# A hybrid decoder step: the chained sum of a gated unit gets a PSUM tile of its own, and its seven products another order

## The chip, the cores and the metric

The kernel runs on one core of one Trainium2 chip. Its time is the device time of one execution in microseconds; a kernel is run several times and the median counts. TensorE (matmuls), VectorE, ScalarE, GpSimd and SyncE (transfers) each work through a queue of their own in order, and wait for each other with semaphores. TensorE writes its sums to PSUM, which has eight banks; VectorE and ScalarE read them there.

## What is computed

One step of a trunk of two layers for 560 tokens (16 meta tokens, 32 of running sequences, 512 of a new prompt), in float32. The model is 1024 wide, the hidden width is 2816:

```python
def swiglu(x, w_gate, w_up, w_down):
    return (jax.nn.silu(x @ w_gate) * (x @ w_up)) @ w_down
...
for l in range(DEPTH):
    h = h + 0.5 * swiglu(rmsnorm(h, norm_ffn1[l]), ffn1_w_gate[l], ffn1_w_up[l], ffn1_w_down[l])
    m, a, b, c = mixer(rmsnorm(h, norm_mix[l]), l, ...)   # HGRN2 heads and an S5 state-space part
    h = h + m
    h = h + 0.5 * swiglu(rmsnorm(h, norm_ffn2[l]), ffn2_w_gate[l], ffn2_w_up[l], ffn2_w_down[l])
return rmsnorm(h, norm_final), ...
```

So there are four FFN stages and two mixers: FFN, mixer, FFN, FFN, mixer, FFN.

## The kernel before, in words

Every float32 product is made of three products of reduced-precision halves: a value is split into a high part and the rest, and high x high, high x low and low x high are summed (`mms`, line 397; the matmuls `mm<-xh,wh`, `xl,wh`, `xh,wl` of the profile). The low part of a weight comes from a copy with the sign turned and a transfer that adds the weight from HBM onto it (`wl<-in_gu_dram` on GpSimd's queue).

An FFN stage has 22 units of 128 hidden features each (`Unit`, line 804). Gate and up product of a unit together are a 2 x 2 block product over halves of the tokens and halves of the inputs, done with seven block products in place of eight (`PROD`, line 801; the operands are sums and differences that `t_wsum` and `Norm.t_blocks` make). Each of the seven is 12 matmuls of 280 columns (272 in the last stage): four groups of three. The sums 1, 6, 7 and 4 are one chain in bank 0 of the unit's tile `x` (`mm` in the profile, two banks): after 1, 6 and 7 ScalarE copies the running sum to SBUF (`t_cuts`, line 841: `s1`, `u2`, `u3`), and the next product adds on to it in place. Products 5 and 3 are a second chain in bank 1 of the same tile, with the copy `s5` between them. Product 2 has a one-bank tile `c` of its own (`m` in the profile). `t_hid` (line 851) puts gate (`f`, tile `fa`) and up (`b`, tile `s`) together, multiplies them by the row scale of the norm, applies Silu, multiplies and splits.

The order of TensorE's products is written out in `ffn` (line 984): within a unit 6, 2, 3, 7, then products 1 and 5 of the next unit, then 4. After each chunk of 4 or 6 units (`CH`) the down product of the chunk follows: eight output tiles, each 24 matmuls for a chunk of four, with `t_res` (VectorE, `h<-mm,h`) adding the result to `h`.

All else is a list scheduler in Python that runs when the kernel is built (`Sched`, line 131). Tasks are generators that yield operations; the scheduler keeps estimated clocks, knows each operation's estimated cost, and emits the operation with the earliest start, with a pull by the task's priority and a `slack` that holds back a task's operations. What it emits is each engine's program order; the semaphores are then put in by the framework. For the tiles of two PSUM banks it kept its dependences per bank (`keys`, line 87, and `Pool.banks`). PSUM tiles come from two pools: `mm`, three tiles of two banks (`am()`), and `m1`, two tiles of one (`am1()`); a task that asks for a tile waits for a free one.

Two other tasks matter here. `Norm.t_sum` makes the row scale of a stage (squares on ScalarE, sums on VectorE or GpSimd, `rstd_of`, line 652); it runs while the first units are already on TensorE. `t_setup(l)` (line 1116) computes the S5 tables of layer l on the side, with low priority, during the FFN stages; the S5 part of the mixer (`t_s5`) sends `u` through HBM (`su<-u`, `ut<-su`) only once that setup is done (`yield d.ev`), and `x0` in the mixer's order waits for all four S5 outputs.

Of the kernel before, what the change touches and what calls it, by code (L numbers as in the profile page):

```python
# [12 lines left out]
AF = mybir.ActivationFunctionType  # L13
# [70 lines left out]
        self.pool, self.w, self.dt, self.name = pool, w, dt, name  # L84


def keys(a):

    n = a.tensor.name
    if a.ap[0][0] != 1024 or a.space != PSUM:  # L90
        return [n]
    lo = a.offset % 1024
    hi = lo + sum(st * (c - 1) for st, c in a.ap[1:])
    return [f"{n}/{b}" for b in range(lo // 512, hi // 512 + 1)]


class Op:
    __slots__ = ("eng", "cost", "outs", "ins", "fn", "lat", "alt", "bias", "port")

    def __init__(self, eng, cost, outs, ins, fn, lat=None, port=False):  # L100
        self.eng, self.cost, self.fn, self.alt, self.bias = eng, cost, fn, None, 0.0

        self.port = port
        self.lat = LAT[eng] if lat is None else lat
        self.outs = [n for a in outs for n in keys(a)]
        self.ins = [n for a in ins for n in keys(a)]


class Pool:
    def __init__(self, tp, shape, n, tag):  # L110
        self.tp, self.shape, self.tag = tp, shape, tag
        self.free = [0.0] * n
        self.n = n
        self.banks = tag == "gmm"


class Task:
# [13 lines left out]
class Sched:  # L131
# [20 lines left out]
    def free(self, *aps):  # L152
        for a in aps:
            n = a.tensor.name
            p = self.owner.pop(n)
            if n in self.wnames:
                self.wnames.discard(n)
                self.wheld -= 1
            ks = [n, f"{n}/0", f"{n}/1"] if p.banks else [n]
            p.free.append(max(d.get(k, ("", 0.0))[1] for k in ks for d in (self.wt, self.rt)))  # L160

    def step(self, t, val=None):
        try:
# [27 lines left out]
    def settle(self):  # L191
        again = True
        while again:
            again = False
            for t in list(self.tasks):
                while t in self.tasks:
                    c = t.cur
                    if c is None and not t.started:
                        self.step(t)
                    elif isinstance(c, Ev):  # L200
                        if not c.done:
                            break
                        self.step(t)
                    elif isinstance(c, Req):
                        p = self.pools[c.pool]
                        if len(p.free) <= self.reserve(t, c.pool):
                            break
                        p.free.sort()
                        tm = p.free.pop(0)
                        if c.pool == "a" and t.need:  # L210
                            t.took += 1
                        if c.pool == "a" and t.weights is not None:
                            self.wheld += 1
                        ap = p.tp.tile(p.shape, c.dt, tag=p.tag, name=c.name)
# [4 lines left out]
                        for k in [n, f"{n}/0", f"{n}/1"] if p.banks else [n]:  # L219
                            self.rt[k] = ("", tm)  # L220
# [48 lines left out]
    def run(self):  # L269
        self.settle()  # L270
        while self.tasks:
            best = {}
            for t in self.tasks:
# [10 lines left out]
                        o.alt.alt = None  # L284
                b = best.get(o.eng)
                key = st + PULL.get(o.eng, 0.0) * t.prio
                if t.slack and o.eng == "PE":
                    key = max(key, rdy + t.slack)
                if b is None or key < b[2] - 1e-9:
                    best[o.eng] = (st, t, key)  # L290
# [9 lines left out]
def hymba(ctx: ExitStack, tc: tile.TileContext, *aps):  # L300
# [35 lines left out]
    def tt(o, a, b, op, eng=None):  # L336
        if eng is ANY:
            return flex(tt(o, a, b, op), tt(o, a, b, op, G))
        e = eng or V
        c = nel(o) * 1.04 + 65 if e is V else nel(o) * 2.1 + 147  # L340
        return Op("V" if e is V else "G", c, [o], [a, b], lambda: e.tensor_tensor(o, a, b, op=op), port=sb(a, b))  # L341

    def flex(a, b, bias=BIAS):
# [305 lines left out]

    def rstd_of(acc, n, T=TOK):
        W = T // 2
        ps = yield am1()
        accs = acc if isinstance(acc, list) else [acc]
        yield mms([(ps[64 * j:64 * j + 64, 0, :W], ones, a[:, W * j:W * (j + 1)], a is accs[0], a is accs[-1])
                   for a in accs for j in range(2)])
# [21 lines left out]
        rs = yield al("rs", w=T)  # L679
        S = T // 2 if T > NH else T  # L680
        for o in range(0, T, S):
            ps = yield am1()
# [9 lines left out]
    class Norm:  # L692
        def __init__(self, nm, l, src, ev, o0=0):
# [9 lines left out]
            else:  # L703
                self.xs = [Ev() for _ in range(KD)]
                spawn(self.t_split(), 2.931, name="split" + nm)
            spawn(self.t_sum(), 8.533, name="sum" + nm).slack = 1500.0 if self.fast else 0.0

        def source(self, k):
            if self.src[k] is None:
# [62 lines left out]
        def t_sum(self):  # L772
            acc = None
            for k in range(KD):
# [5 lines left out]
                    yield add(q, q, acc, ANY)  # L780
                    free(acc)
                acc = q
            self.rs.val = yield from rstd_of(acc, D, self.T)
            self.rs.done = True

        def drop(self):
# [16 lines left out]

    class Unit:
        def __init__(self, nrm, f, k):
            self.i = unit_at[f, k]
            self.nrm, self.W = nrm, nrm.T // 2
            self.x = self.c = None
            self.pe = [Ev() for _ in range(8)]
            self.got = {k: Ev() for k in ("s1", "s5", "u2", "u3")}  # L810
            self.left = {"G": 2, "A": 2, "B": 2, "U": 1}
            self.out = Ev()

        def prod(self, j):
            w, o, b = PROD[j]
            q, i = wq[self.i], self.i
            if j == 1:
                self.x = yield am()
                spawn(t_cuts(self), 2.45, name="cuts")
                spawn(t_hid(self), 2.452, name="hid")  # L820
            if j == 2:
                self.c = yield am1()
            wait = {6: "s1", 3: "s5", 7: "u2", 4: "u3"}.get(j)
            if wait:
                yield self.got[wait]
            yield q.done[w]
            wh, wl, tiles = q.val[w]
            out = self.c[:, 0, :self.W] if j == 2 else self.x[:, 1 if j in (3, 5) else 0, :self.W]
            onto = wait is not None
            for k in range(4):  # L830
                e = self.nrm.xb[b][k]
# [6 lines left out]
            if not self.left[w]:  # L838
                free(*tiles)

    def t_cuts(t):
        W = t.W
        for j, nm, n, c, o in ((1, "s", "s1", 0, 0), (5, "s", "s5", 1, W), (6, "u", "u2", 0, 0), (7, "u", "u3", 0, W)):
            yield t.pe[j]
            if o == 0:
                t.val = yield al(nm, w=2 * W)
                setattr(t, nm, t.val)
            yield acopy(t.val[:, o:o + W], t.x[:, c, :W])
            t.got[n].done = True

    def t_hid(t):
        T, W = t.nrm.T, t.W
        a_, b_ = slice(0, W), slice(W, T)
        yield t.pe[2]
        f = yield al("fa", w=T)
        yield add(f[:, a_], t.c[:, 0, :W], t.s[:, a_])
        free(t.c)
        yield t.pe[3]
        yield add(f[:, b_], t.x[:, 1, :W], t.u[:, a_])
        yield t.nrm.rs  # L860
        rs = t.nrm.rs.val
        yield mul(f, f, rs)
        yield act(f, f, AF.Silu)
        yield t.got["u3"]
        b = t.s
        yield add(b[:, b_], t.u[:, b_], b[:, b_])
        free(t.u)
        yield mul(b[:, b_], b[:, b_], rs[:, b_])
        yield t.pe[4]
        yield mul(b[:, a_], t.x[:, 0, :W], rs[:, a_])  # L870
        free(t.x)
        yield mul(f, f, b)
        free(b)
        t.out.val = yield from split(f)
# [109 lines left out]
    def ffn(nrm, f, nm2, l2=0):  # L984
        us = [Unit(nrm, f, k) for k in range(FT)]
        prog = []
        for u in range(FT):
            if not u or u in ends:
                prog += [(u, 1), (u, 5)]
            if u + 1 in ends:  # L990
                prog += [(u, j) for j in (6, 2, 7, 3, 4)] + [(None, ends.index(u + 1))]
            else:
                prog += [(u, j) for j in ((2, 6, 3, 7) if u == 0 else (6, 2, 3, 7))] + [(u + 1, 1), (u + 1, 5), (u, 4)]
        hids = [u.out for u in us]
        for u, j in prog:
            if u is not None:
# [119 lines left out]
    def t_setup(l):  # L1116
# [76 lines left out]
        ps = yield am1()  # L1193
        yield trs([(ps[:, 0, 0:128], q8)])
        qt = small("qt", 128)
        yield acopy(qt, ps[:, 0, 0:128])
# [62 lines left out]
        pw = [bc[:, 512:1024], p1[:, 0:512], p1[:, 512:1024], p2[:, 0:512], p2[:, 512:1024]]  # L1259
        for n in range(4):  # L1260
            yield from cmul16(pw[n + 1], ar, ai, pw[n])
        ht, zt = xt[:, 0:512], xt[:, 512:1024]
        ps = yield am1()
        for mt in range(4):
            for c in range(2):
# [9 lines left out]
                yield mms([(ps[32 * jj:32 * jj + 32, 0, 128 * mt:128 * mt + 128],  # L1275
                            be[:, 512 * c + 128 * mt + 32 * jj:512 * c + 128 * mt + 32 * jj + 32],
                            ce[:, 160 * jj:160 * jj + 128], c == 0, c == 1) for jj in range(4)])
        free(bc, p1, p2, be)
        yield acopy(ht, ps[:, 0])
        free(ps)  # L1280
# [11 lines left out]
        free(xt)  # L1292

        es = [small(f"es{n}", 32) for n in range(10)]
        yield vcopy(es[0], un)
# [653 lines left out]
```

## Time and profile before

| | |
|---|---|
| median of 3 runs | 2375.29 us (2368.11 to 2376.02) |
| profiled execution | 2368.96 us, span 2367.2 us |
| TensorE busy | 2123.0 us, 17370 matmuls |
| TensorE's mean granted clock | 0.976 of full speed |

The span is what the profiler saw of the execution; 1.8 us lie around it. In the rows below times are microseconds, of one instruction nanoseconds; "PE" is TensorE's matmuls, "PEld" its weight loads, DVE VectorE, ACT ScalarE, POOL GpSimd, SPq SyncE's queue. `mm<-xh,wh` means: the instruction writes tile `mm` and reads `xh` and `wh`. "[0.61 <-DVE fa]" is idle time just before the instruction and what ended it. In the timelines each row begins with its start and its duration, and neighbours of one kind are merged (x12).

### The profile page before, as it was taken

Reading aid. Unit: us, or ns where it says so; the run is one execution under the profiler, and the core shown is the slowest. Engines: PE = TensorE matmul, PEld = TensorE weight load, DVE = VectorE, ACT = ScalarE, POOL = GpSimd, SP = SyncE. Lnnn points to the kernel's source line nnn. Section 1 sums busy time; section 2 is a strip of 40 time slices with the busy share of each in tenths; the row PEclk is TensorE's granted clock in tenths of the full one; section 3 lists DMA queues with packets and bytes.
Section 4 is the critical chain, followed back from the end, with each engine's and each line's share of the span. In section 5 each row is a group of like instructions: output and inputs, shape, how many; then the busy total and the mean of one; then the engine's idle time right before and its main releaser. Section 6 shows DMA issues by size and latency. Waiting matters only on the chain.

```text
span 2367.2 us, 43934 instructions
## 1 busy us (share of the span) xinstructions
PE 2123.0 (90%) x17370; PEld 2029.0 (86%) x17370; DVE 1632.5 (69%) x3647; ACT 1171.7 (49%) x1898; POOL 522.4 (22%) x623
## 2 busy tenths in 40 slices
PE   5899999998799899999979999999988989999997
PEld 4888898997689898989979988889878888888987
DVE  8867767868568876856888765555677776556564
ACT  6455555443355544565554554454425455544553
POOL 3122222322222122223221211112311231111111
PEclk9999999999899999999999999999989999999998
DMA  6677776986566567776747775678855647656663
GB/s 180 136 192 173 165 202 157 230 238 175 126 153 160 140 148 205 174 178 173 178 99 173 191 173 138 142 171 223 217 145 131 173 103 172 160 144 143 157 142 87
DMA packets 153615, 388.63 MB, mean 164 GB/s; under 512 B 16208, under 2 KB 36464, under 8 KB 153408
## 3 DMA queue, kind: packets, MB, share of 16 engines
q0 software_dynamic: 66048, 177.80, 39.7%
q1 hardware_dynamic: 75904, 182.48, 23.9%
q10 hardware_dynamic: 11456, 25.54, 3.1%
q8 instruction: 136, 2.23, 0.4%
q14 instruction: 71, 0.58, 0.1%
HBM read 353.08 MB, written 32.67 MB: 163 GB/s over the span
## 4 chain that ended last, share of the span: by engine, by line
PE 75%; DVE 12%; ACT 5%; issue 3%; DMA 3%; POOL 1%; SPq 0%; DVEq 0%; ACTq 0%; POOLq 0%
PE mm L416 68%; PE m L416 7%; DVE fa L341 2%; ACT s L380 2%; DVE xl L341 1%; ACT wh L380 1%; DMA ut<-su 1%; DVE qp L341 1%; DMA su<-u 1%; DVE w L1392 1%; DVE w L341 1%; DVE rv L341 1%; DVE wr L341 1%; DVE wl L341 1%; ACT wl L380 1%
## 5 line engine op out<-in xcount | busy, mean ns | idle before, releaser
L416 PE MATMUL mm<-xh,wh 128*128 128x280 f32 (+1 forms) x4128 | 1048.9, 300 | 122.8 <-ACT s L380 58.1
L416 PE MATMUL mm<-xh,wl 128*128 128x280 f32 (+1 forms) x4128 | 1017.6, 293 | 11.7 <-DVE wl L341 5.9
L416 PE MATMUL mm<-xl,wh 128*128 128x280 f32 (+1 forms) x4128 | 1018.8, 293 | 3.6 <-DVE xl L341 3.5
L416 PEld LDWEIGHTS mm<-xh,wh 128*128 128x128 f32 x4128 | 712.8, 190 | 178.7 <-ACT s L380 81.4
L416 PEld LDWEIGHTS mm<-xh,wl 128*128 128x128 f32 x4128 | 714.6, 190 | 12.4 <-DVE wl L341 6.3
L416 PEld LDWEIGHTS mm<-xl,wh 128*128 128x128 f32 x4128 | 715.0, 190 | 5.4 <-DVE xl L341 5.3
L380 ACT ACTIVATE wh<-wr 128x1024 fp32r<-128x1024 f32 (+2 forms) x596 | 528.6, 913 | 278.7 <-DVE wr L341 168.9
L380 ACT ACTIVATE wl<-wr 128x1024 fp32r<-128x1024 f32 (+1 forms) x244 | 249.2, 1021 | 38.1 <-PE mm L416 20.2
L341 DVE TENSOR_TENSOR wr<-wr 128x512 f32<-128x512 f32 x352 | 245.7, 698 | 23.7 <-ACT wh L380 21.0
L341 DVE TENSOR_TENSOR wl<-wr,wh 128x1024 fp32r<-128x1024 f32 x176 | 214.6, 1220 | 64.8 <-ACT wh L380 33.3
L369 DVE SCALAR_TENSOR_TENSOR h<-mm,h 128x560 f32<-128x560 f32 (+1 forms) x157 | 115.1, 735 | 134.5 <-PE mm L416 133.8
L395 POOL DMA_DIRECT2D wl<-in_gu_dram x88 | 76.5, 869 | 572.5 <-ACT wl L380 398.8
L395 POOL DMA_DIRECT2D wl<-in_dn_dram x96 | 103.6, 1079 | 395.4 <-ACT wl L380 215.2
L380 ACT ACTIVATE s<-mm 128x280 f32<-128x280 f32 (+2 forms) x184 | 75.2, 411 | 188.5 <-PE mm L416 178.1
L416 PE MATMUL mm<-x,wh 128*128 128x280 f32 (+1 forms) x1056 | 155.0, 293 | 12.3 <-DVE fa L341 11.3
L380 ACT ACTIVATE u<-mm 128x280 f32<-128x280 f32 (+1 forms) x176 | 70.5, 400 | 182.0 <-PE mm L416 166.8
L416 PEld LDWEIGHTS mm<-x,wh 128*128 128x128 f32 x1056 | 141.3, 188 | 17.7 <-DVE fa L341 15.9
L341 DVE TENSOR_TENSOR fa<-mm,u 128x280 f32<-128x280 f32 (+1 forms) x88 | 39.3, 447 | 114.9 <-PE mm L416 96.8
L416 PE MATMUL m<-xh,wh 128*128 128x280 f32 (+1 forms) x352 | 103.6, 294 | 6.2 <-ACT xh L380 5.0
L341 DVE TENSOR_TENSOR s<-mm,rs 128x280 f32<-128x280 f32 (+1 forms) x88 | 39.1, 445 | 101.4 <-PE mm L416 101.3
L395 POOL DMA_DIRECT2D wh<-in_gu_dram x88 | 77.2, 877 | 134.0 <-ACT wh L380 111.6
L416 PE MATMUL m<-xl,wh 128*128 128x280 f32 (+1 forms) x352 | 103.5, 294 | 1.7 <-DVE xl L341 1.7
(301 smaller groups left out, 2417.9 us busy)
## 6 DMA issues: line engine op xcount, KB each, us to landing
wr<-in_gu_dram SPq DMA_DIRECT2D x176, 512.0 KB, 5.4
wl<-in_gu_dram POOLq DMA_DIRECT2D x88, 512.0 KB, 5.7
wr<-in_dn_dram SPq DMA_DIRECT2D x64, 512.0 KB, 4.8
wl<-in_dn_dram POOLq DMA_DIRECT2D x64, 512.0 KB, 8.6
wh<-in_gu_dram POOLq DMA_DIRECT2D x88, 256.0 KB, 5.7
wr<-in_win_dram SPq DMA_DIRECT2D x40, 512.0 KB, 6.2
wl<-in_win_dram POOLq DMA_DIRECT2D x40, 512.0 KB, 8.1
wr<-in_dn_dram SPq DMA_DIRECT2D x32, 384.0 KB, 3.7
```

Source lines behind the costliest of these rows:

```text
L341: return Op("V" if e is V else "G", c, [o], [a, b], lambda: e.tensor_tensor(o, a, b, op=op), port=sb(a, b))
L369: lambda: V.scalar_tensor_tensor(o, a, s, b, op0=op0, op1=op1), port=sb(a, b))
L380: return Op("S", nel(o) * 0.833 + (190 if sc else 95 if sb(a) else 60), [o], [a] + sc, lambda: S.activation(o, a, func, scale=scale, **kw))
L395: return Op("G", 900.0, [o], [i, o], lambda: G.dma_start(o, i, accum_op=ALU.add), lat=-n / 240.0)
L416: PE.matmul(out, lhsT=lhsT, rhs=rhs, start=st, stop=sp_, **kw)
L1392: yield vop(a, [a, d.r4], lambda a=a, dk=dk: V.tensor_tensor_scan(a, dk, a, 0.0, op0=ALU.mult, op1=ALU.add))
```

## The change

The chain 1, 6, 7, 4 moves to a one-bank tile of the pool `m1`. Products 5 and 3 (bank 0) and 2 (bank 1) share a two-bank tile of `mm`, taken at product 5. The order in a unit is now 6, 3, 7, 2 (the first unit of a stage keeps 2, 6, 3, 7; the last of a chunk has 6, 3, 7, 2, 4). `t_cuts` and `t_hid` follow: `u2` is copied into the tile of `f`, `u3` into that of `b`, and the sum with product 3 comes before that with product 2. In the first two units of a stage the last sum of the chain is copied to SBUF before the row scale is waited for. The scheduler's dependences are per tile again, its cost of a GpSimd sum goes up, slack holds for ScalarE as for TensorE, `t_hid` gets a slack of 400 ns, and the square sums of the FFN stages get priority 1.9 in place of 8.533. `rstd_of` of the FFN norms and the setup's matmuls take their PSUM tile from `mm`; the setup takes one for each of four blocks and copies each block out, into `bc`.

```diff
-def keys(a):
-
-    n = a.tensor.name
-    if a.ap[0][0] != 1024 or a.space != PSUM:
-        return [n]
-    lo = a.offset % 1024
-    hi = lo + sum(st * (c - 1) for st, c in a.ap[1:])
-    return [f"{n}/{b}" for b in range(lo // 512, hi // 512 + 1)]
...
-        self.outs = [n for a in outs for n in keys(a)]
-        self.ins = [n for a in ins for n in keys(a)]
+        self.outs = [a.tensor.name for a in outs]
+        self.ins = [a.tensor.name for a in ins]
...
-                if t.slack and o.eng == "PE":
+                if t.slack and o.eng in ("PE", "S"):
                     key = max(key, rdy + t.slack)
...
-        c = nel(o) * 1.04 + 65 if e is V else nel(o) * 2.1 + 147
+        c = nel(o) * 1.04 + 65 if e is V else nel(o) * 2.4 + 150
...
-    def rstd_of(acc, n, T=TOK):
+    def rstd_of(acc, n, T=TOK, bank=am1):
...
-            spawn(self.t_sum(), 8.533, name="sum" + nm).slack = 1500.0 if self.fast else 0.0
+            spawn(self.t_sum(), 1.9 if self.fast else 8.533, name="sum" + nm).slack = 1500.0 if self.fast else 0.0
...
-            self.rs.val = yield from rstd_of(acc, D, self.T)
+            self.rs.val = yield from rstd_of(acc, D, self.T, am if self.fast else am1)
...
             if j == 1:
-                self.x = yield am()
+                self.x = yield am1()
                 spawn(t_cuts(self), 2.45, name="cuts")
-                spawn(t_hid(self), 2.452, name="hid")
-            if j == 2:
-                self.c = yield am1()
+                spawn(t_hid(self), 2.452, name="hid").slack = 400.0
+            if j == 5:
+                self.c = yield am()
...
-            out = self.c[:, 0, :self.W] if j == 2 else self.x[:, 1 if j in (3, 5) else 0, :self.W]
+            out = self.c[:, 1 if j == 2 else 0, :self.W] if j in (2, 3, 5) else self.x[:, 0, :self.W]
...
     def t_hid(t):
         T, W = t.nrm.T, t.W
         a_, b_ = slice(0, W), slice(W, T)
+        yield t.got["u2"]
+        yield t.pe[3]
+        yield add(t.f[:, b_], t.c[:, 0, :W], t.f[:, b_])
         yield t.pe[2]
-        f = yield al("fa", w=T)
-        yield add(f[:, a_], t.c[:, 0, :W], t.s[:, a_])
+        yield add(t.f[:, a_], t.c[:, 1, :W], t.s[:, a_])
         free(t.c)
-        yield t.pe[3]
-        yield add(f[:, b_], t.x[:, 1, :W], t.u[:, a_])
-        yield t.nrm.rs
-        rs = t.nrm.rs.val
-        yield mul(f, f, rs)
-        yield act(f, f, AF.Silu)
+        f = t.f
+
+        rs = None
+        if t.k > 1:
+            yield t.nrm.rs
+            rs = t.nrm.rs.val
+            yield mul(f, f, rs)
+            yield act(f, f, AF.Silu)
...
-                prog += [(u, j) for j in (6, 2, 7, 3, 4)] + [(None, ends.index(u + 1))]
+                prog += [(u, j) for j in (6, 3, 7, 2, 4)] + [(None, ends.index(u + 1))]
             else:
-                prog += [(u, j) for j in ((2, 6, 3, 7) if u == 0 else (6, 2, 3, 7))] + [(u + 1, 1), (u + 1, 5), (u, 4)]
+                prog += [(u, j) for j in ((2, 6, 3, 7) if u == 0 else (6, 3, 7, 2))] + [(u + 1, 1), (u + 1, 5), (u, 4)]
...
-        ht, zt = xt[:, 0:512], xt[:, 512:1024]
-        ps = yield am1()
+        ht, zt = bc[:, 0:512], xt[:, 512:1024]
         for mt in range(4):
+            ps = yield am()
...
+            yield acopy(ht[:, 128 * mt:128 * mt + 128], ps[:, 0, 0:128])
+            free(ps)
```

## Rows read from the trace of the kernel before

**Rows 1.** The page: busy time of each engine over the span.

```profile
PE 2123.0 (90%) x17370; PEld 2029.0 (86%) x17370; DVE 1632.5 (69%) x3647; ACT 1171.7 (49%) x1898; POOL 522.4 (22%) x623
```

**Rows 2.** The page: the chain that ended last, by engine.

```profile
PE 75%; DVE 12%; ACT 5%; issue 3%; DMA 3%; POOL 1%; SPq 0%; DVEq 0%; ACTq 0%; POOLq 0%
```

**Rows 3.** List of waits, whole span: who waited for whom: us, times, longest.

```profile
ACT u L380 <- PE mm L416: 166.8, 120, 4.1
...
DVE fa L341 <- PE mm L416: 96.8, 77, 3.9
...
PEld mm L416 <- ACT s L380: 81.4, 102, 6.7
...
PEld mm L416 <- DVE fa L341: 62.1, 76, 1.2
...
PEld mm L416 <- ACT u L380: 22.4, 32, 0.8
```

**Rows 4.** Timeline of TensorE in the third FFN stage: starts of groups.

```profile
1450.95 0.29 PE L416 MATMUL mm<-xh,wh 128*128 128x280 f32 x1
...
1455.97 0.29 PE L416 MATMUL mm<-xh,wh 128*128 128x280 f32 x1
1457.12 0.40 PE L416 MATMUL mm<-xh,wh 128*128 128x280 f32 x1 [0.61 <-DVE fa L341]
...
1459.55 0.29 PE L416 MATMUL mm<-xh,wh 128*128 128x280 f32 x1
1460.59 0.40 PE L416 MATMUL mm<-xh,wh 128*128 128x280 f32 x1 [0.49 <-ACT s L380]
...
1470.48 0.29 PE L416 MATMUL mm<-xh,wh 128*128 128x280 f32 x1
...
1473.06 0.40 PE L416 MATMUL mm<-xh,wh 128*128 128x280 f32 x1 [0.49 <-ACT s L380]
```

**Rows 5.** Timeline of VectorE, the same stretch.

```profile
1456.62 0.45 DVE L341 TENSOR_TENSOR fa<-mm,u 128x280 f32<-128x280 f32 x1 [0.61 <-PE mm L416]
...
1457.76 1.22 DVE L341 TENSOR_TENSOR wl<-wr,wh 128x1024 fp32r<-128x1024 f32 x1
```

**Rows 6.** Timeline of ScalarE, the same stretch.

```profile
1460.13 0.40 ACT L380 ACTIVATE s<-mm 128x280 f32<-128x280 f32 x1 [0.96 <-PE mm L416]
1460.43 1.05 ACT L380 ACTIVATE wh<-wr 128x1024 fp32r<-128x1024 f32 x1
```

**Rows 7.** Windows: one chunk; length, busy PE, PEld, DVE, ACT, POOL, clock, DMA.

```profile
1413.87:1490.80 76.93, 71.03 (x528) 68.55 (x528) 43.80 (x67) 37.29 (x54) 11.55 (x12) 1.00 0.64 149
```

**Rows 8.** Timeline of TensorE at the end of that chunk.

```profile
1490.80 0.52 PE L416 MATMUL mm<-xl,wh 128*128 128x280 f32 x2 [0.49 <-DVE xl L341]
```

**Rows 9.** Timeline of TensorE at the starts of two FFN stages.

```profile
75.90 0.60 PE L416 MATMUL mm<-xh,wh 128*128 128x280 f32 x1 [3.58 <-DVE s L341]
...
1208.63 1.20 PE L416 MATMUL m<-sq,ones 128*64 128x280 f32 x4 [7.77 <-POOL sq L341]
```

**Rows 10.** Timeline of VectorE: the first S5 input of each mixer.

```profile
475.41 1.29 DVE L341 TENSOR_TENSOR u<-mm,rs 128x16 f32<-128x16 f32 x4 [0.37 <-PE mm L416]
...
1638.73 1.28 DVE L341 TENSOR_TENSOR u<-mm,rs 128x16 f32<-128x16 f32 x4 [0.37 <-PE mm L416]
```

**Rows 11.** Timeline of SyncE's queue: the first S5 transfers of each mixer.

```profile
498.56 14.24 SPq L391 DMA_DIRECT2D su<-u  x12
...
1640.03 1.92 SPq L391 DMA_DIRECT2D su<-u  x4
```

**Rows 12.** Timeline of GpSimd: first and last `sce` transfer of the first setup.

```profile
255.88 0.80 POOL L391 DMA_DIRECT2D sce<-cx  x1 [5.45 <-DVE wr L341]
...
335.32 0.79 POOL L391 DMA_DIRECT2D sce<-cx  x1 [6.85 <-ACT cx L380]
```

**Rows 13.** Timeline of GpSimd: the last accumulating gate load of a chunk.

```profile
1451.24 0.85 POOL L395 DMA_DIRECT2D wl<-in_gu_dram  x1 [15.66 <-PE mm L416]
```

**Rows 14.** The page: transfers, with KB each and median us to landing.

```profile
wl<-in_gu_dram POOLq DMA_DIRECT2D x88, 512.0 KB, 5.7
```

More of the change, by code (lines that the diff above doesn't have):

```diff
@@ L113, in __init__ @@
         self.n = n
-        self.banks = tag == "gmm"
 class Task:
@@ L158, in free @@
                 self.wheld -= 1
-            ks = [n, f"{n}/0", f"{n}/1"] if p.banks else [n]
-            p.free.append(max(d.get(k, ("", 0.0))[1] for k in ks for d in (self.wt, self.rt)))
+            p.free.append(max(d.get(n, ("", 0.0))[1] for d in (self.wt, self.rt)))
     def step(self, t, val=None):
@@ L218, in settle @@
                             self.wnames.add(n)
-                        for k in [n, f"{n}/0", f"{n}/1"] if p.banks else [n]:
-                            self.rt[k] = ("", tm)
+                        self.rt[n] = ("", tm)
                         if c.w:
@@ L648, in split @@
         return hi, lo
-    def rstd_of(acc, n, T=TOK):
+    def rstd_of(acc, n, T=TOK, bank=am1):
         W = T // 2
-        ps = yield am1()
+        ps = yield bank()
         accs = acc if isinstance(acc, list) else [acc]
@@ L681, in rstd_of @@
         for o in range(0, T, S):
-            ps = yield am1()
+            ps = yield bank()
             yield mms([(ps[:, 0, j * W - o:j * W - o + W], wb[:, j], a, i == 0, i == 1)
@@ L805, in __init__ @@
         def __init__(self, nrm, f, k):
-            self.i = unit_at[f, k]
+            self.i, self.k = unit_at[f, k], k
             self.nrm, self.W = nrm, nrm.T // 2
@@ L841, in t_cuts @@
     def t_cuts(t):
[L842 to L849, printed above, removed]
+        T, W = t.nrm.T, t.W
+        a_, b_ = slice(0, W), slice(W, T)
+        yield t.pe[1]
+        t.s = yield al("s", w=T)
+        yield acopy(t.s[:, a_], t.x[:, 0, :W])
+        t.got["s1"].done = True
+        yield t.pe[5]
+        yield acopy(t.s[:, b_], t.c[:, 0, :W])
+        t.got["s5"].done = True
+        yield t.pe[6]
+        t.f = yield al("fa", w=T)
+        yield acopy(t.f[:, b_], t.x[:, 0, :W])
+        t.got["u2"].done = True
+        yield t.pe[7]
+        t.b = yield al("fb", w=T)
+        yield acopy(t.b[:, b_], t.x[:, 0, :W])
+        t.got["u3"].done = True
     def t_hid(t):
@@ L853, in t_hid @@
         a_, b_ = slice(0, W), slice(W, T)
+        yield t.got["u2"]
+        yield t.pe[3]
+        yield add(t.f[:, b_], t.c[:, 0, :W], t.f[:, b_])
         yield t.pe[2]
-        f = yield al("fa", w=T)
-        yield add(f[:, a_], t.c[:, 0, :W], t.s[:, a_])
+        yield add(t.f[:, a_], t.c[:, 1, :W], t.s[:, a_])
         free(t.c)
-        yield t.pe[3]
-        yield add(f[:, b_], t.x[:, 1, :W], t.u[:, a_])
-        yield t.nrm.rs
-        rs = t.nrm.rs.val
-        yield mul(f, f, rs)
-        yield act(f, f, AF.Silu)
-        yield t.got["u3"]
[L865 to L871, printed above, removed]
+        f = t.f
[5 more added lines that the diff above has]
+            yield act(f, f, AF.Silu)
+        yield t.got["u3"]
+        b = t.b
+        yield add(b[:, b_], b[:, b_], t.s[:, b_])
+        free(t.s)
+        if rs is None:
+            yield t.pe[4]
+            yield acopy(b[:, a_], t.x[:, 0, :W])
+            free(t.x)
+            yield t.nrm.rs
+            rs = t.nrm.rs.val
+            yield mul(b, b, rs)
+        else:
+            yield mul(b[:, b_], b[:, b_], rs[:, b_])
+            yield t.pe[4]
+            yield mul(b[:, a_], t.x[:, 0, :W], rs[:, a_])
+            free(t.x)
+        if t.k < 2:
+            yield mul(f, f, rs)
+            yield act(f, f, AF.Silu)
         yield mul(f, f, b)
@@ L1191, in t_setup @@
         yield from csq(d.a4[:, 0], d.a4[:, 1], a2[:, 0:16], a2[:, 16:32])
-        ps = yield am1()
+        ps = yield am()
         yield trs([(ps[:, 0, 0:128], q8)])
@@ L1261, in t_setup @@
             yield from cmul16(pw[n + 1], ar, ai, pw[n])
-        ht, zt = xt[:, 0:512], xt[:, 512:1024]
-        ps = yield am1()
+        ht, zt = bc[:, 0:512], xt[:, 0:512]
         for mt in range(4):
+            ps = yield am()
             for c in range(2):
@@ L1274, in t_setup @@
                 yield dma("G", d.ce[mt, :, c], ce[:, 0:640].rearrange("p (j n) -> p j n", j=4)[:, :, 32:160])
-                yield mms([(ps[32 * jj:32 * jj + 32, 0, 128 * mt:128 * mt + 128],
+                yield mms([(ps[32 * jj:32 * jj + 32, 0, 0:128],
                             be[:, 512 * c + 128 * mt + 32 * jj:512 * c + 128 * mt + 32 * jj + 32],
                             ce[:, 160 * jj:160 * jj + 128], c == 0, c == 1) for jj in range(4)])
-        free(bc, p1, p2, be)
-        yield acopy(ht, ps[:, 0])
-        free(ps)
+            yield acopy(ht[:, 128 * mt:128 * mt + 128], ps[:, 0, 0:128])
+            free(ps)
+        free(p1, p2, be)
         for mt in range(4):
@@ L1291, in t_setup @@
                           ht[32 * jj:32 * jj + 32].rearrange("p (m q) -> p m q", m=4)[:, :, 0:w])
-        free(xt)
+        free(xt, bc)
         es = [small(f"es{n}", 32) for n in range(10)]
```

## The prediction

> **What bounds the kernel now.** I read the page first. TensorE is busy for 90% of the span and has 75% of the chain that ended last [rows 1, 2]; no other engine comes near. So the question is what TensorE waits for. The list of waits gives three rows that stand out [rows 3]: the weight loads of the `mm` tiles sat idle 81.4 us for ScalarE's copy `s`, 62.1 us for VectorE's sum `fa` and 22.4 us for ScalarE's copy `u`, 165.9 us in 210 waits. All of `s`, `u`, `fa` belong to the gated units. I use the weight-load rows, not the matmul rows: a matmul's end is modelled and overlaps the next, so its idle time is too short.
>
> The timeline says what kind of waits these are [rows 4]. In the undisturbed stretch 1450.95 to 1455.97 thirteen groups of three matmuls start in 5.02 us: 0.1287 us a matmul, so 84 for one unit should take 10.81 us. From 1460.59 to 1473.06 a unit takes 12.47 us, 1.66 us more, and there are just two gaps in it. The first: product 7 has issued two groups (the second starts at 1455.97), then stops until 1457.12, right at the end of `fa`, which ran from 1456.62 for 0.45 us [rows 5]. That sum reads bank 1 of `x`; product 7 writes bank 0. The second: product 5 has issued one group (1459.55) and stops until 1460.59, right at the end of the copy `s`, 1460.13 for 0.40 us [rows 6]. That copy reads bank 0, product 5 writes bank 1. And the copy itself did not start when product 1 was done (its last group starts before 1459.55) but 0.32 us after the last matmul of product 5's first group started (1459.55 + 2 x 0.1287 = 1459.81). Neither side needs the other's bank; each waits because both banks are one tile. The planner, with its keys per bank, believed that they don't wait.
>
> Here a rule of the Trainium skill is weighed. "PSUM — Partial Sum Buffer", section on bank collisions, says that PSUM is to be guarded by bank, and that access to different banks doesn't collide. By that rule the gaps could not come from the neighbour bank, the change would remove none, and the time would stay. The rows above say that this program guards by tile; that is why I don't follow it, and it is the third rival.
>
> **What is removed.** Of the 102 waits for `s`, those of the usual kind have the 0.72 us of a weight load's gap (0.49 us in the matmul row of 1460.59, plus 0.23 because the next load was due earlier): 73.4 us, which leaves 8.0 us in a few long ones (up to 6.7), real waits for data. I keep these. So 165.9 - 8.0 = 158 us are waits for a neighbour bank, about 0.75 us each, 1.8 us for each of the 88 units. As a check, a chunk of four units with its down product holds 528 matmuls, 68.0 us at 0.1287, and takes 76.93 [rows 7]: 9 us lost in four units.
>
> In the new order a unit's chain (products 1, 6, 7, 4) has its own bank and tile. Its copies are followed by other products before the chain goes on: `s` by 5 and 4 of the unit before, `u2` by 3, `u3` by 2. In the other tile, 5 and 3 write bank 0 and 2 writes bank 1. Only two neighbours are left: the sum `fa` of product 3 against product 2, and, in the first unit of a stage alone, the copy of product 5 against 2. So the usual stall should go: **-158**.
>
> **What it puts in their place.** (a) Two slots are now tight. A product lasts 12 x 0.1287 = 1.54 us. The copy `u2` after 6 takes about 0.32 + 0.40 + 0.06 = 0.78 us (delay, copy and restart, [rows 4, 6]) and must be done when 3 ends: 0.76 us to spare. The sum after 3 takes 0.32 + 0.45 + 0.05 = 0.82 and must be done when 7 ends: 0.72 us to spare. Queued ahead can be a weight copy of 1.05 us on ScalarE [rows 6] or a weight difference of 1.22 us on VectorE [rows 5]. Today VectorE reached that `fa` early and waited for TensorE 77 times in 88, ScalarE reached `u` early 120 times in 176 [rows 3]. Behind a late `u2` stands product 7 and all of TensorE; behind a late sum stands product 2. If 15 to 30% of the units meet 0.5 to 1 us, that is 0.2 us a unit: **+18** (bounds 0 and one usual stall in every unit, 70).
>
> (b) Chunk ends. There TensorE already waits for the last hidden tile (the `xl` gap at 1490.80 [rows 8]). VectorE's and ScalarE's way from the last-but-one product to that `xl` is not shortened, so where product 4 no longer stalls, TensorE reaches this wait earlier. About 0.5 us at each of 16 chunk ends that precede a short down product: **+8** (0 to 12).
>
> (c) Stage starts. The square sums get an earlier priority and slack on ScalarE, their sums another PSUM pool; a unit's `c` no longer waits for the row scale, and the first two units copy their last sum out before the scale is there. Before, TensorE stood 7.77 us for a `sq` sum at 1208.63, and 3.58 us at 75.90 for the last reader of a bank that had to wait for the scale [rows 9]. Of the four starts I take about these two waits: **-12** (0 to 25). The extra copy per early unit (0.40 us, 8 units) lies on ScalarE, 49% busy, and VectorE has one multiply of 560 for two of 280: nothing. If ScalarE were full, 3 us.
>
> (d) The first mixer. Its S5 part can't begin before `t_setup(0)` is done. In the second mixer, where setup is long over, the first `su` transfer follows the first `u` by 1.30 us (1638.73, 1640.03); in the first it follows by 23.15 (475.41, 498.56), twelve transfers in one burst [rows 10, 11]. Setup runs on VectorE's spare time, not on TensorE's. So when the first FFN ends some 35 us earlier (158 / 4 less its share of (a)), the mixer's gate moves little, and `x0`, which needs all four S5 outputs, holds main. Less crowded transfers should give some back. **+22** (0 to 40). Setup now takes a two-bank buffer four times for some 20 us (the first setup's eight `sce` transfers run from 255.88 to 335.32, two to a hold [rows 12]) and leaves main two of three; a down product of 24 matmuls, 3.1 us, lies between a buffer's last matmul and its next use, so nothing, at worst 1 us a chunk. Its four small copies for one add about 1 us each to its chain; this lies in (d).
>
> (e) GpSimd's higher cost in the planner moves some sums to VectorE. Which, and what that does to the two mixers, no row shows: 0, bounds -15 and +15.
>
> Sum: -158 + 18 + 8 - 12 + 22 = -122 on the profiled execution's own 2369.0 us (span 2367.2), 2247. The median of the runs is 6 us above that execution; I add half: **2250 us**.
>
> **The rivals.**
> 1. *The weights become the bound.* TensorE would use weights 10% faster. Against it: the last accumulating load for the fourth unit of a chunk is issued at 1451.24 and lands some 5.7 us later [rows 13, 14], while that unit's product 1 starts at 1470.48 [rows 4]: 13.5 us early. The DMA share is 0.64 [rows 7]. Buffers come free sooner too. It binds if the lead shrinks by all of this; I would then get half the gain, about 2310.
> 2. *The tight slots stall in most units* (a at its upper bound): 2250 + 52 = 2302. For it: both helpers are planned with estimates, and a sum that is planned into product 2 stalls it as before.
> 3. *The waits don't go*: the guard is by bank, or the new neighbours meet as often as the old. Time 2369, give or take 10.
> 4. *Slower.* Product 2 stands behind VectorE's queue: with two weight differences ahead of the sum (2.44 us, less the 0.72 to spare, plus 0.25 restart) a unit loses 2.0 us, 176 us in all, in place of the 18 of (a): 2408. It decides from a mean of 1.6 us a unit. Against it, VectorE waited for `fa`'s product 77 times in 88, and is 57% busy in the steady chunk (43.80 of 76.93).
> 5. *A worse plan around setup and the mixers*: all of the first FFN's gain lost and 15 us in the mixers: 2285.
>
> **How the numbers follow.** The forecast 0.64 (its own range 2215 to 2280); weights 0.08; tight slots 0.11; no change 0.05; slower 0.04; worse plan 0.08. The low end lets (a), (b) and (d) be nearly nothing and (c) its best: 2369 - 158 - 20 + 5 = 2196. The high end takes in rivals 2 and 5 and most of rival 1: 2310. Outside lie no change, slower, half of rival 1 and the tails, under 2 in 10. About 0.5%, 12 us, is what this measurement tells from no change: faster 0.91 (forecast, rivals 1, 2 and 5), same 0.05, slower 0.04.
>
> **What would show it.** Right: the three rows of waits fall from 166 us to under 50; the steady unit takes 11.0 us or less; the chunk 69 to 71; PE busy time stays near its level while the span falls; `su` in the first mixer still starts around 490 to 505 with TensorE idler before it. Wrong: gaps of 0.5 us or more ahead of products 7 or 2 in most units (rival 2, 4), waits for `wl`, `wh` or DMA in the steady chunk (rival 1), gaps in product 5 as before (rival 3).

## The result, and the profile after

The changed kernel takes 2179.97 us (median, 2179.2 to 2182.45) against 2372.83 for the kernel before beside it: a ratio of 0.919, 95% interval 0.9171 to 0.921. That is 193 us less, where the prediction had 122; 2250 was 70 us too high, and the time lies 16 us under the low end of the range. The profiled span is 2177.4 us, 189.8 us shorter. Lines have moved: 403 is now the matmul, 328 the VectorE sum, 367 the ScalarE copy.

The page of the changed kernel, busy time of each engine, answers to [rows 1]; under it the chain that ended last, for [rows 2]:

```profile
PE 2063.0 (95%) x17370; PEld 2012.4 (92%) x17370; DVE 1629.0 (75%) x3656; ACT 1161.6 (53%) x1907; POOL 495.6 (23%) x611
...
PE 76%; DVE 14%; DMA 4%; issue 3%; ACT 3%; POOL 0%; SPq 0%; ACTq 0%; DVEq 0%; POOLq 0%
```

The same 17370 matmuls stand in a shorter span: TensorE went from 90% to 95% busy. Its busy time fell by 60 us with no matmul removed, most of it, by an estimate below, because a stall lengthens the busy time of the matmuls on both sides of it. The mean granted clock is 0.983 of full speed, where it was 0.976; in the steady chunks of [rows 7] and below it is 1.00, the upper of its two levels (2.4 GHz), in both kernels, so the clock has no part in the steady units. Over the whole span it can be worth at most some 20 us of the 190 (an estimate: 0.024 of 2367.2 us against 0.017 of 2177.4).

The list of waits of TensorE's weight loads in the changed kernel (who waited for whom: us in total, times, longest), which answers to [rows 3]:

```profile
PEld mm L403 <- ACT wh L367: 12.7, 3, 12.4
...
PEld mm L403 <- DVE xl L328: 7.0, 9, 1.2
...
PEld mm L403 <- ACT s L367: 4.3, 2, 3.4
...
PEld m L403 <- ACT fa L367: 2.2, 5, 0.9
PEld mm L403 <- DVE fa L328: 2.0, 5, 0.7
```

The three rows of before, 165.9 us in 210 waits, have become 6.3 us in 7: `s` twice and `fa` five times. The copy `u` of before is now ScalarE's `fa`, with 2.2 us in 5. No row of that size has taken their place (the rows by `issue`, where the profile shows nothing that was waited for, are 54.7 us and were 57.1 before). The largest row left that names a releaser is nearly all one wait of 12.4 us, at 29.5 us, for ScalarE's copy of an early weight; the kernel before waited 6.7 us for `s` at 23.6. The timeline of TensorE in the changed kernel's third FFN stage (start, duration) shows a unit without a stall, beside [rows 4]:

```profile
1333.78 1.73 PE L403 MATMUL m<-x,wh 128*128 128x280 f32 x12
1335.35 0.29 PE L403 MATMUL m<-xh,wh 128*128 128x280 f32 x1
...
1344.65 1.72 PE L403 MATMUL m<-x,wh 128*128 128x280 f32 x12
1346.21 0.29 PE L403 MATMUL m<-xh,wh 128*128 128x280 f32 x1
```

No row from one `x12` to the next has a bracket of idle time, and the unit takes 10.86 us (1335.35 to 1346.21) where it took 12.47. A chunk of four units in this stage, in the windows of the changed kernel (length, busy PE, PEld, DVE, ACT, POOL, clock, DMA), answers to [rows 7]:

```profile
1252.21:1321.57 69.36, 68.43 (x530) 68.20 (x529) 43.73 (x67) 37.12 (x55) 11.63 (x13) 1.00 0.76 175
```

It lasts 69.36 us in place of 76.93. The DMA share rose from 0.64 to 0.76, and no wait for weights lies in that chunk. What the prediction said of the first mixer came out otherwise. These rows are the first `u`, the first `su` behind it and the setup's last transfer `stt`, in the timelines of VectorE, SyncE's queue and GpSimd ([rows 10, 11] have the first two before; `stt` stood at 512.83 there).

```profile
432.11 1.26 DVE L328 TENSOR_TENSOR u<-mm,rs 128x16 f32<-128x16 f32 x4
...
442.70 1.77 SPq L378 DMA_DIRECT2D su<-u  x2
...
455.94 0.56 POOL L378 DMA_DIRECT2D stt<-ti  x1
```

`su` was to stand still near 498. It moved 56 us, more than the 43 us by which `u` moved.

### The profile page after: what moved, and what is told of

Its sections match the earlier page's. It is cut to its first block, busy times and chain, and to the rows that moved or that the text cites. A ratio compares the mean times of both kernels' runs of the same rounds, so it can differ in the third digit from the quotient of the medians.

```text
span 2177.4 us, 43853 instructions
## 1 busy us (share of the span) xinstructions
PE 2063.0 (95%) x17370; PEld 2012.4 (92%) x17370; DVE 1629.0 (75%) x3656; ACT 1161.6 (53%) x1907; POOL 495.6 (23%) x611
## 4 chain that ended last, share of the span: by engine, by line
PE 76%; DVE 14%; DMA 4%; issue 3%; ACT 3%; POOL 0%; SPq 0%; ACTq 0%; DVEq 0%; POOLq 0%
PE mm L403 52%; PE m L403 23%; DVE xl L328 2%; DVE wr L328 1%; DVE w L328 1%; DVE wl L328 1%; DMA wl<-in_dn_dram 1%; ACT wh L367 1%; DVE qp L328 1%; DMA su<-u 1%; DVE fa L328 1%; DVE rv L328 1%; DMA wr<-in_gu_dram 1%; DMA ut<-su 1%; DVE w L1404 1%
## 5 line engine op out<-in xcount | busy, mean ns | idle before, releaser
L403 PE MATMUL mm<-xh,wh 128*128 128x280 f32 (+1 forms) x3424 | 820.7, 295 | 22.1 <-ACT wh L367 12.1
L403 PE MATMUL mm<-xl,wh 128*128 128x280 f32 (+1 forms) x3424 | 809.6, 292 | 5.1 <-DVE xl L328 5.1
L403 PE MATMUL mm<-xh,wl 128*128 128x280 f32 (+1 forms) x3424 | 808.0, 291 | 5.3 <-DVE wl L328 4.5
L403 PEld LDWEIGHTS mm<-xh,wh 128*128 128x128 f32 x3424 | 575.9, 189 | 37.6 <-ACT wh L367 12.4
L403 PE MATMUL m<-xh,wh 128*128 128x280 f32 (+1 forms) x1056 | 309.8, 293 | 9.1 <-DVE kx8r L356 7.5
L403 PE MATMUL m<-xh,wl 128*128 128x280 f32 (+1 forms) x1056 | 308.2, 292 | 6.2 <-DMA wl<-in_gu_dram 6.2
L403 PE MATMUL m<-xl,wh 128*128 128x280 f32 (+1 forms) x1056 | 308.2, 292 | 1.0 <-DVE xl L328 0.9
L328 DVE TENSOR_TENSOR wl<-wr,wh 128x1024 fp32r<-128x1024 f32 x176 | 214.9, 1221 | 54.7 <-ACT wh L367 33.1
L403 PEld LDWEIGHTS m<-xh,wh 128*128 128x128 f32 x1056 | 199.7, 189 | 12.2 <-ACT sq L367 7.5
L403 PEld LDWEIGHTS m<-xh,wl 128*128 128x128 f32 x1056 | 199.5, 189 | 6.7 <-DMA wl<-in_gu_dram 6.7
L403 PEld LDWEIGHTS m<-xl,wh 128*128 128x128 f32 x1056 | 200.0, 189 | 1.7 <-DVE xl L328 1.7
L403 PE MATMUL m<-x,wh 128*128 128x280 f32 (+1 forms) x1056 | 149.7, 291 | 0.0
```

Of the source, the lines that this page charges most:

```text
L403: PE.matmul(out, lhsT=lhsT, rhs=rhs, start=st, stop=sp_, **kw)
```

## The experiments

The table cuts each profiled execution at VectorE's last sum into `h` of every stage (F an FFN stage, M a mixer; some 30 us after F3 are the same in all). `gap` is from the first `u` to the first `su`, `setup` the start of the first setup's last `stt`. All in us, but for `ahead`: the first setup ends with 192 VectorE operations that make its last tables (tiles `tr`, `ti`, `tm`), and this is how many of them stand ahead of F0's last sum in VectorE's order.

| kernel | median | F0 | M0 | F1 | F2 | M1 | F3 | gap | setup | ahead |
|---|---|---|---|---|---|---|---|---|---|---|
| before | 2372.83 | 461.7 | 311.7 | 431.1 | 420.5 | 307.3 | 404.4 | 23 | 513 | 41 |
| changed | 2179.97 | 417.6 | 307.4 | 385.7 | 382.7 | 298.1 | 355.3 | 11 | 456 | 64 |
| e9_tiles_alone | 2202.64 | 430.7 | 303.1 | 389.6 | 383.6 | 308.6 | 355.9 | 10 | 468 | 88 |
| e3_old_tiles | 2289.29 | 450.7 | 292.7 | 416.9 | 407.5 | 296.5 | 388.4 | 1 | 471 | 136 |
| e2_old_order | 2191.66 | 419.0 | 317.7 | 393.0 | 379.9 | 296.2 | 354.0 | 23 | 470 | 38 |
| e5_no_extras | 2215.31 | 424.5 | 313.3 | 395.2 | 380.5 | 311.8 | 358.2 | 23 | 476 | 34 |
| e10_prio_slack_old | 2202.97 | 423.9 | 315.8 | 392.7 | 381.7 | 302.1 | 357.7 | 23 | 475 | 33 |
| e6_gpsimd_cost_old | 2188.75 | 421.1 | 303.0 | 393.2 | 379.8 | 304.6 | 354.0 | 11 | 459 | 66 |
| e4_after_bankkeys | 2194.92 | 423.2 | 306.1 | 396.9 | 383.8 | 296.4 | 355.9 | 11 | 462 | 64 |
| e8_setup_late | 2189.91 | 418.7 | 320.4 | 387.8 | 383.6 | 296.3 | 353.4 | 30 | 478 | 0 |
| e7_setup_early | 2170.78 | 430.7 | 294.5 | 385.9 | 382.5 | 296.2 | 353.1 | 1 | 406 | 192 |
| e12_setup_mid | 2173.48 | 416.7 | 304.2 | 387.3 | 381.2 | 295.6 | 354.8 | 13 | 453 | 96 |
| e11_before_setup_early | 2358.54 | 471.5 | 293.7 | 431.7 | 420.2 | 310.5 | 403.9 | 1 | 439 | 192 |

**The tiles alone** (e9): the new tiles, with the old order, the scheduler's old dependences per bank, and the old priority, slack and GpSimd cost (two of its cuts are shown).

```diff
-                prog += [(u, j) for j in (6, 3, 7, 2, 4)] + [(None, ends.index(u + 1))]
+                prog += [(u, j) for j in (6, 2, 7, 3, 4)] + [(None, ends.index(u + 1))]
...
-        c = nel(o) * 1.04 + 65 if e is V else nel(o) * 2.4 + 150
+        c = nel(o) * 1.04 + 65 if e is V else nel(o) * 2.1 + 147
```

> One part of the change alone: the new tiles (chain in a bank of its own, products 5, 3 and 2 in one two-bank tile, first two units copied out early), with the old order of products and the old planner (dependences per bank, old priorities, slack and GpSimd cost). Theory A (the tiles take the waits away, and setup and mixers follow at the FFN stages' pace): the waits for s, u and fa nearly vanish, the first mixer is not longer than before by more than 5 us, 2205 to 2245. Theory B (the planner's true dependences are needed for the gain): waits for a neighbour bank remain, 2260 to 2330. The forecast's step on the first mixer (its gate stands still) would make the first mixer 20 us longer than before.

2202.64 us, ratio 0.9284 (0.926 to 0.9307): 170 of the 193 us. The four FFN stages lose 157.9 us. The usual waits for `s` and `fa` are gone here too, in the list of weight-load waits of this kernel:

```profile
PEld mm L416 <- DVE xl L341: 9.5, 14, 1.4
PEld mm L416 <- POOL sq L341: 8.3, 1, 8.3
...
PEld mm L416 <- ACT s L380: 5.3, 5, 2.3
```

The 8.3 us for `sq` is the stage-start wait of [rows 9], which only the changed settings remove.

**The old tiles in the changed kernel** (e3): chain and products 5 and 3 share a two-bank tile again, 2 has one of its own, and the row scale and the setup take their PSUM from `m1` as before (one cut of several).

```diff
-            out = self.c[:, 1 if j == 2 else 0, :self.W] if j in (2, 3, 5) else self.x[:, 0, :self.W]
+            out = self.c[:, 0, :self.W] if j == 2 else self.x[:, 1 if j in (3, 5) else 0, :self.W]
```

> The changed kernel with the old tiles: the chain 1, 6, 7, 4 and the products 5 and 3 share a two-bank tile again, product 2 has a one-bank tile, the row scale and the setup take their PSUM from the pool they had; order of products and planner as changed. Theory A: the waits for a neighbour bank return, at least 1.5 a unit of 0.75 us, 100 us or more: 2280 to 2380. Theory B: only part of the gain goes, 2210 to 2260.

2289.29 us, 0.965 (0.9632 to 0.9668). The waits come back, in the list of this kernel:

```profile
PEld mm L403 <- DVE fa L328: 54.6, 43, 2.2
PEld mm L403 <- ACT fa L367: 34.4, 46, 1.5
PEld mm L403 <- ACT s L367: 28.2, 26, 3.2
```

That is 117.2 us in 115 waits, and the FFN stages are 122 us longer than in the changed kernel. So the tiles are the cause, and the list of weight-load waits gives nearly the price of them; the new order on the old tiles has fewer such meetings, but dearer ones (1.02 us a wait against 0.79). Yet this kernel is 84 us faster than the kernel before that ran beside it, with the old tiles: its FFN stages are 54 us shorter, M0 19 and M1 11. So the shares overlap: the tiles are worth 170 us where they come alone (e9) and 109 where they come last (e3).

**The old order in the changed kernel** (e2):

```diff
-                prog += [(u, j) for j in (6, 3, 7, 2, 4)] + [(None, ends.index(u + 1))]
+                prog += [(u, j) for j in (6, 2, 7, 3, 4)] + [(None, ends.index(u + 1))]
...
-                prog += [(u, j) for j in ((2, 6, 3, 7) if u == 0 else (6, 3, 7, 2))] + [(u + 1, 1), (u + 1, 5), (u, 4)]
+                prog += [(u, j) for j in ((2, 6, 3, 7) if u == 0 else (6, 2, 3, 7))] + [(u + 1, 1), (u + 1, 5), (u, 4)]
```

> The changed kernel with the products in the order of before (6, 2, 3, 7; at chunk ends 6, 2, 7, 3, 4), tiles and planner as changed. Theory A with the order as a needed part: product 3 then writes bank 0 beside the sum that reads product 2 in bank 1, a wait of 0.75 us in most units comes back, 66 us: 2235 to 2255. Theory A with the tiles alone doing it: both sums of the hidden part come after 2 and 3 are both written, so nothing reads beside a write, and u2 has two products of cover: within 10 us of 2180. Theory B: within 15 us of 2180.

2191.66 us, 0.9232 (0.9215 to 0.9249), 12 us more than the changed kernel; but F2 and F3 are no longer (379.9 and 354.0 against 382.7 and 355.3). The 12 us lie in M0 (10) and F1 (7). The 10 go with the setup's place (`gap` is 23 again). The order keeps nothing apart in the steady units that the tiles don't. What planning the old tiles with dependences per tile alone would do stays open: the run meant for it (e1, the kernel before with that one edit) gave no time, and e3 has it together with the order and the settings.

**The settings of the scheduler.** e5 puts all four back (priority 1.9 of the square sums, slack for ScalarE, slack 400 of `t_hid`, GpSimd's cost), e10 the first three, e6 the last, e4 brings back the dependences per bank.

```diff
-                if t.slack and o.eng in ("PE", "S"):
+                if t.slack and o.eng == "PE":
...
-            spawn(self.t_sum(), 1.9 if self.fast else 8.533, name="sum" + nm).slack = 1500.0 if self.fast else 0.0
+            spawn(self.t_sum(), 8.533, name="sum" + nm).slack = 1500.0 if self.fast else 0.0
...
-                spawn(t_hid(self), 2.452, name="hid").slack = 400.0
+                spawn(t_hid(self), 2.452, name="hid")
...
-        c = nel(o) * 1.04 + 65 if e is V else nel(o) * 2.4 + 150
+        c = nel(o) * 1.04 + 65 if e is V else nel(o) * 2.1 + 147
```

> The changed kernel without the planner's side changes: square sums at priority 8.533, slack for TensorE alone, no slack for the hidden part, GpSimd's sum at its old cost. Theory A: these touch neither the tiles nor the order of the products; 2175 to 2200. Theory B: a good part of the gain beyond the forecast comes from them, by way of the stage starts, the setup and the mixers: 2210 to 2250.

> The changed kernel with the old priority and slack (square sums at 8.533, slack for TensorE alone, none for the hidden part) and GpSimd's new cost. With both undone it was 2215, with the cost alone undone 2189. If priority and slack give the stage starts and the cost gives the mixers, 2190 to 2205: stages as in the kernel with both undone, mixers near the changed kernel's. If either alone brings most of it, 2180 to 2192.

> The changed kernel with GpSimd's sum at its old cost in the planner (2.1 ns an element) and nothing else. If the 35 us that the planner's side changes gave together lie in the mixers by way of this cost, 2195 to 2210, with the two mixers longer by 15 to 20 us together and the FFN stages as in the changed kernel; if priority and slack gave them, 2175 to 2190 and the mixers as in the changed kernel.

> The changed kernel with the planner's dependences per bank as before; tiles, order and the rest as changed. Theory A: with the new order a read and a write of neighbour banks hardly meet, so the planner's wrong belief costs little; 2175 to 2200. Theory B: 2210 to 2260.

Ratios 0.9336 (0.9322 to 0.9351), 0.928 (0.9267 to 0.9293), 0.9227 (0.9206 to 0.9249) and 0.9255 (0.9239 to 0.9271): 35, 23, 9 and 15 us more than the changed kernel. That the four settings hardly matter (2175 to 2200) was wrong. Without the four settings the FFN stages are 17 us longer, F0 (7) and F1 (9.5) above all. M1 is 302 to 305 with one part of the settings old, 309 and 312 with all old (e9, e5), and 296 to 298 with all new, on the old tiles of e3 too: its 9 us come from the settings, not from tiles or order. M0 follows no single edit, but it follows `gap` over the whole table: 293 to 295 us where `gap` is 1, 303 to 307 at 10 to 13, 312 to 318 at 23, 320 at 30.

**The first setup's place.** e8 lets the first setup begin later, e7 and e12 raise its priority in the changed kernel, e11 in the kernel before.

```diff
-        yield wev0[2]
+        yield wev0[16 if l == 0 else 2]
```

```diff
-spawn(t_setup(0), 8.527, name="setup")
+spawn(t_setup(0), 3.0, name="setup")
```

(6.0 in e12.)

> The changed kernel with the first setup held until the load of the seventh unit's gate weights (second unit's now), so that it starts some 60 us later. If setup goes at the pace of VectorE's queue and not of its spare time, its last table leaves 40 to 60 us later than in the changed kernel (455.9), near 500 to 515, the first su transfer follows the first u by 50 to 75 us, and the first mixer gets 20 to 50 us longer: 2200 to 2230. This is also the size of what the forecast feared. If setup catches up in spare time, its end moves by under 20 us and the time stays within 10 us of 2180.

> The changed kernel with the first setup at priority 3.0 in place of 8.527, so that its tables are there before the first mixer asks. If the gate at the mixer's start still costs what the gap there shows (first u at 432.1, first su at 442.7, 11 us), the gap closes, the first mixer gets 5 to 15 us shorter and the time is 2165 to 2178, less what VectorE's earlier setup work costs the first FFN stage. If the mixer's length is set elsewhere, 2178 to 2190.

> The changed kernel with the first setup's priority half way (6.0 in place of 8.527; 3.0 gave 2171). Theory (place in the queue): the setup ends between 406 and 456; if it ends before the first FFN does, the mixer has its 13 us and the first FFN loses less than the 13 it lost at 3.0: 2160 to 2172. Rival (any setup work moved ahead costs the FFN what the mixer gets): 2168 to 2185.

> The kernel before, with the first setup alone moved up in priority (8.527 to 3.0). Theory (the setup's place in the queues sets its end, and the gate it is for the first mixer costs some 13 us in either kernel): the setup ends ahead of the first FFN's end, the first u is followed by su within 2 us, the first mixer falls from 311.7 to some 295 to 300, the first FFN grows by about as much as in the changed kernel (13), total 2360 to 2375. Rival (setup runs in VectorE's spare time, which the old kernel's TensorE stalls give it, and the gate stands where that time ends): the setup still ends behind the first FFN, after 470, and the mixer stays at 308 to 315.

e8, 0.9231 (0.9214 to 0.9248): the setup's first VectorE work began at 106.8 us in place of 35.3, its end came only 22.5 us later, between the two forecasts (40 to 60, and under 20), and M0 grew by 13 us. e7, 0.9144 (0.913 to 0.9158), and e12, 0.9166 (0.9151 to 0.9181), have medians 9.2 and 6.5 us under the changed kernel's. The interval of e7 lies below that kernel's (0.9171 to 0.921), that of e12 overlaps it, so its 6.5 us may be nothing. In e7 M0 gains 13 us and F0 loses as much; its gain shows as a few us in M1 and F3. In e12 the setup ended hardly earlier (453), so a gain, if there is one, is not the setup's.

e11 tells most: 0.9941 (0.9918 to 0.9964), 12 us under the kernel before that ran beside it, with all its bank waits left in. The same three points, in the timelines of VectorE, SyncE's queue and GpSimd of e11:

```profile
485.30 1.27 DVE L341 TENSOR_TENSOR u<-mm,rs 128x16 f32<-128x16 f32 x4 [0.37 <-PE mm L416]
...
486.60 1.77 SPq L391 DMA_DIRECT2D su<-u  x4
...
438.66 0.93 POOL L391 DMA_DIRECT2D stt<-ti  x1
```

With TensorE as slow as before, the setup ended 74 us earlier than in the kernel before (512.83) and 33 us ahead of the FFN stage's end, `su` followed `u` by 1.30 us, and M0 fell by 18 us; F0 grew by 10. So the old kernel could have had its tables in time, at that price; the setup was late because of where it stands in the queues.

How the setup holds `su` back stands in the waits of SyncE's queue (before, 488.2 to 498.6; changed, 430.9 to 442.8; e11, 467 to 487):

```profile
SPq L391 <- DVE ti L341: 10.0, 1, 10.0
...
SPq L378 <- DVE ti L328: 11.4, 1, 11.4
...
SPq L391 <- DVE u L341: 19.5, 1, 19.5
```

In the two kernels the first `su` stands right behind a weight load of the mixer in that queue, and the load waits for `ti`, a table of the setup, whose tiles come from the same pool as the weights' (`aa`). In e11 only `u` itself is waited for.

## Why the prediction was right in kind and 70 us too high

Against the span's own change of 189.8 us each term of the sum stands so:

| term | predicted | measured | read from |
|---|---|---|---|
| waits for a neighbour bank | -158 | about -165 (estimate) | unit 12.47 to 10.86, two waits: 0.80 each, x 205 of the 210 |
| (a) tight slots | +18 | about +4 | weight-load waits for the two `fa` |
| (b) chunk ends | +8 | +2 to +4 | waits for `xl`, 5.3 before; 7.0 changed, 9.5 tiles alone |
| FFN stages, the three together | -132 | -158 | e9, FFN stages |
| (c) stage starts | -12 | -18, with all else of the change | FFN stages, changed kernel against e9 |
| (d) first mixer | +22 | -4 | M0 |
| (e) GpSimd's cost, mixers | 0 | -9 | M1 |
| sum | -122 | -190 | |

**The mechanism was right.** The guard is by tile, and the wait for a neighbour bank was the loss: new tiles alone remove it (e9), old tiles bring it back (e3), and unit and chunk (10.86 and 69.36) lie where the prediction put them. Rival 3 falls. The Trainium skill, "PSUM — Partial Sum Buffer", section "PSUM bank collisions raise a hardware error", lets a program guard by bank. The trace disagrees with reading this program so: its framework waits for the whole tile, 0.80 us for each such wait, where by that rule the time would have stayed near 2369.

**Step (d) failed, the largest single part of the miss** (26 of 68 us; the FFN stages with (c) make 32, (e) 9). The prediction said that the setup "runs on VectorE's spare time, not on TensorE's", so that "the mixer's gate moves little". The gate was real: taking it away is worth 18 us in the kernel before (M0 of e11) and 13 in the changed one (M0 of e7). But it moved: the setup's end went from 513 to 456, as far as the FFN stage's end went and 13 us more. e11 shows that spare time did not set it, since with the old TensorE and a higher priority it ended at 439. The setup's operations stand behind FFN operations in queues that are worked through in order; when the FFN operations ahead of them stop waiting, they come sooner. Counted in VectorE's order, 799 other operations stand ahead of the setup's last table operation before and 793 in the changed kernel, so its place hardly moved while all that is ahead of it took 57 us less. `gap` follows that order in every run (column `ahead`): 23 where 33 to 41 table operations stand ahead of F0's last sum, 10 to 13 with 64 to 96, 1 with 136 or all, 30 with none. e8 shows that their own start doesn't set it either (71 us later there, 22 later here). Seen in the trace alone, e9, e2, e5 and e10 say the same: the setup ends 24 to 38 us after the first `u` in all of them, as in the two kernels. Which estimates of the scheduler put it there was not tried. So the sign that the prediction named for this step, a first `su` near 490 to 505, failed too.

**(a) was priced as a chance and hardly came** (14 us). The prediction gave 15 to 30% of the units a stall of 0.5 to 1 us. The waits for the copy after 6 and the sum after 3 are ten, 4.2 us in all, in 88 units. Both helpers had 0.7 us to spare, and in the rows of before they had mostly been early; that evidence was there and was given too little weight. Rivals 2 and 4, which hang on the same slots, fall with it.

**The price of a wait was 0.75 and is 0.80** (7 us). The matmul row shows 0.61 or 0.49 us of idle time at a stall, 0.55 in the mean. The rest sits in busy time, by an estimate from the timeline of [rows 4]. The last matmul before a stall counts with its whole 0.29 us and not with the 0.13 after which the next would start, 0.16 us more. The one that restarts takes 0.40 us where the others take 0.29, and the next follows it after 0.24 us (1469.20 to 1469.44) and not 0.13, 0.11 us more. That makes 0.82 us a stall, close to the 0.80 of the whole units, and 55 of the 60 us by which TensorE's busy time fell; the prediction had wanted it to stay near its level. The two gaps that the prediction describes (1457.12, 1460.59) lie ahead of the 12.47 us that it measures; inside are two of the same kind, at 1469.20 and 1473.06, so the number holds.

**(b), (c)** had the right sign; how much of the 18 us is (c) isn't shown. The wait of 3.9 us at 75.90 is gone with the tiles alone, and so lies in the -158. The one for `sq` (8.0 us; 8.3 in e9, 8.8 in e5) goes with the settings, but it stands at the start of F2, and 13 of the 18 us lie in F0. There a wait in the first 30 us grew instead, from 6.7 (7.6 in e9) to 12.4 us. Both waits of [rows 9] also lie in stretches of half clock (70.2 to 80.4 and 1203.5 to 1213.7: granted clock 0.50, the lower level, 1.2 GHz), which the changed kernel hasn't at these two starts, so idle time alone does not price them. **(e)** lay within its bounds of 15: M1 is 9 us shorter by the scheduler's settings. Both e6 and e10 give part of it (6.5 and 4 us); which instructions moved stays open. Rival 5 went the other way.

**Rival 1** (weights) didn't come: the share of the DMA rose to 0.76 as TensorE used the weights faster, and the waits for `wl<-in_gu_dram` in the weight loads are 6.7 us in 2, of which one of 6.2 us is the first weights of the whole kernel:

```profile
PEld m L403 <- DMA wl<-in_gu_dram: 6.7, 2, 6.2
```

That row is from the changed kernel's list of waits; the one before had 6.1 us in one such wait.

## What to carry to other kernels

Look for waits between engines that share a tile and no data: with this framework, two accumulators in one tile cost a stall each time that one is read while the other is written, and the difference of a whole unit (with and without a gap) prices it better than the idle time. Background work that stands in the same in-order queues moves with the foreground; before calling a gate fixed, count what stands ahead of it in its queue, raise its priority in the old kernel, as e11 did, and see whether it moves. Where a list scheduler plans the rest, a small edit elsewhere moves other stages by 10 us either way, so cut the span by stage before crediting an edit with the total.

## What the runs showed that was not expected

TensorE's busy time is no constant of the work: 17370 matmuls are 2123.0 us in one kernel and 2063.0 in the other. The reorder that the change sets out to make is worth nothing in the steady units once the tiles are apart; together with the old dependences, the old order was even 13 us better under the old settings (e9 against e5), and with the new dependences 12 worse under the new (e2 against the changed kernel). In both, 10 us of it are M0 and go with `gap` (10 against 23, 23 against 11): what looked like an effect of the order is where the first setup came to stand.
